# Hybrid decoder layer on one core: residual additions queued behind the local softmax's maxima, local scores in another order, other places for the attention steps

## The chip, the core and the metric

The kernel runs on one core of a Trainium2 chip. The core has five engines that work side by side, each with its own queue of instructions: TensorE (PE, matrix products; its weight loads are shown as PEld), VectorE (DVE), ScalarE (ACT), GpSimd (POOL), and SyncE (SP), which here only issues transfers. [...] Semaphores order the engines among each other. The metric is the device time of one execution in microseconds (us), as the median of several runs.

## The reference

One layer of a hybrid decoder on 4096 new prompt tokens (width 1024) and 8 x 8 sample tokens with caches. Cut to what matters here:

```
h = rmsnorm(x, g_pre);  z = h @ w_in          # 2816 columns: conv, q, k, v, gates
out_a = silu(cg) * cb * conv3(cc * ch)        # 256 columns
# window attention: 8 query heads, 2 key heads, blocks of 128 queries,
# keys of this and of the previous block, a sink logit per head
s = q k^T / 8, masked to the last 128 keys;  m = max(max(s), sink)
p = exp(s - m) / (sum(exp(s - m)) + exp(sink - m));  out_b = silu(ag) * (p v)
# cross attention: 4 heads, 256 memory tokens
out_c = silu(mg) * (softmax(mq mk^T / 8) mv)
y = concat(out_a, out_b, out_c) @ w_out       # 1024 x 1024
x + rmsnorm(y, g_post)
```

Everything is in float32. The kernel keeps this exactness by splitting factors into a high and a low part of the fast float32 format and adding three products (two where it suffices).

## The kernel before

The work has two stages. The first, some 938 us long, is the input projection in three phases over groups of output columns; each phase goes through eight token blocks of 520, each block through seven products of a Strassen scheme (`steps`, line 505). In the third phase the attention of the first chunk (256 tokens) runs between the products, cut in pieces that are taken one per step: `third_jobs` (line 812) gives the step n = 7(b-1)+p its jobs, n = 14 makes the memory's keys (`mem_keys`, whose transposes stand in a PSUM tile until lines 809 and 810 have read it), n = 15 loads chunk 0 (`first_chunk`, line 840), and from n = 16 on one piece of the list `third["chunk"]` is taken per step. The first piece is `chunk.values` (line 849), the transposes of V (line 1117, `vtp`), then come the four head pairs of window and cross attention. When the list is empty, chunk 1 is loaded.

The second stage is the output projection of 33 blocks of 128 tokens (`Block.run`, line 1548): two accumulators `y` of 512 columns, for each of them eight steps of three products (line 1561). Before the products of a step, `starts` may call something (line 1559): here the attention of the later chunks is woven in. A half-block h (128 tokens, chunk h // 2) has two parts. `first_half(h)` (line 1592) takes the window scores (`window_scores`, line 1283: 16 products `ws`, eight over all 128 rows at line 1292, then eight over 64 rows at line 1295), the transposes `xt` of the half-block before (line 1326), then the window softmax of both key heads (`window_probabilities`, line 1299), and it issues loads: for an even h the keys, queries and V of the chunk after (`chunk_load`: ten transfers on GpSimd's queue, one on SP's), for an odd one the gates of the next chunk (`load_mix`, SP). `second_half(h)` (line 1607) takes the memory scores `xs`, the value products `wo` of the half-block before, for an even h V's transposes, then the transposes `wt` of the window probabilities (line 1338), which ScalarE copies (line 1270) and GpSimd masks (lines 1275 and 1278).

The window softmax of a key head is, on VectorE if nothing else is said: copy of the scores (ScalarE, line 1305), masking with the scores of the block before (1306), maximum (1247), its negative with the sink (1249) and the sink's share (1251), exponentials with sums (ScalarE, 1255), sum (1257), reciprocal (1259), multiplication (1260). Both heads go through it one after the other.

Where the parts stand is written in `EARLY` (line 1630) as steps counted from the first block, 16 per block: first and second half of half-block 2 at 4 and 12, of 3 at 14 and 20, of 4 at 22 and 28, of 5 at 30 and 36, and the first half of 6 at 38. From then on every block has a second half at its step 12, and from block 3 on a first half at step 4.

At the end of a block its norm is made: squares (ScalarE, 1569), the sum on VectorE (1574), a power on GpSimd (1575), and the residual on VectorE (1579), which scales `yn`, adds the block's input `xr` in place, and is followed by the store (1580). `yn` has one buffer, `xr` two: the load of a block's rows waits for the store of the block two before.

In this stage TensorE's order is the program's order. The other engines' order is made by a planner, which goes through the work with its own estimate of times and takes, among what it thinks ready, what stands first in the program. `keep_in_program_order(x)` pins x behind the instruction that was written just before it for the same engine.

Of the kernel before, what the change touches and what calls it, by code (L numbers as in the profile page):

```python
# [15 lines left out]
P = 128  # L16
# [36 lines left out]
def hybrid_layer(ctx: ExitStack, tc: tile.TileContext, a: dict):  # L53
# [786 lines left out]
    def first_chunk():  # L840

        mem_stack.close()
        third["work"] = mem_stack.enter_context(tc.tile_pool(name="work", bufs=5, side="right"))
        chunk_load(0)
        chunk = chunks[0]
        chunk.load_mix()
        third["chunk"] = pieces = [lambda: chunk.values(None)]
        for left, right_, both in chunk.pairs():
            pieces += [lambda u=u, n=n: [next(u, None) for _ in range(n)] for n in (2, 1) for u in (left, right_)] + [both]
# [208 lines left out]

    class Chunk:
# [185 lines left out]
        def window_softmax(self, b, kvh, sm):  # L1245
            mx = tiny.tile([P, 4], F32, tag="mx", name=f"wmx{b}_{kvh}")
# [7 lines left out]
            for hh in range(4):  # L1254
                S.activation(sm[:, hh, :], sm[:, hh, :], AF.Exp, bias=nm[:, hh : hh + 1], scale=SCALE,  # L1255
                             accum_out=den[:, hh : hh + 1])
            V.tensor_tensor(den, den, es, op=ALU.add)
# [25 lines left out]
        def window_scores(self, i):  # L1283
            b = 2 * self.c + i
            w = [two_banks("w", f"ws{b}_{kvh}") for kvh in range(2)]
            tasks = [(kvh, j % 2, j // 2) for kvh in range(2) for j in range(4)]
            out = lambda kvh, col, bank: w[kvh][:, bank, 256 * col : 256 * col + 256]
            q = lambda kvh, col, bank: self.q[:, 4 + 2 * (2 * bank + col) + kvh, i * P : i * P + P]
            k = lambda kvh, part: self.kst[:, 2 * kvh + part, i * P : i * P + 2 * P]
            for kvh, col, bank in sorted(tasks):  # L1290

                TE.matmul(out(kvh, col, bank), q(kvh, col, bank), k(kvh, 0), start=col == 0, stop=True, skip_group_check=col > 0)
            for kvh, col, bank in sorted(tasks):
                r = slice(64 * bank, 64 * bank + 64)
                TE.matmul(out(kvh, col, bank), q(kvh, col, bank)[r], k(kvh, 1)[r], start=False, stop=True,
                          skip_group_check=True, tile_position=(64 * bank, 0))
            self.ws = w

        def window_probabilities(self, i):
            b, w = 2 * self.c + i, self.ws  # L1300
            self.sms = []
            for kvh in range(2):
                sm = work([P, 4, P], "sm", f"sm{b}_{kvh}")
# [3 lines left out]
                self.window_softmax(b, kvh, sm)  # L1307
                self.sms.append(sm)
# [212 lines left out]
    class Block:  # L1521
# [26 lines left out]
        def run(self, last, starts):  # L1548
# [6 lines left out]
            for p, (c0, c1) in enumerate(parts):  # L1555
                acc = psum("z", f"y{b}_{p}")[:, : c1 - c0]
                j, passes = 0, 3 if m == P else 2
                for k in range(KT):
                    starts.get((p, k), lambda: None)()
                    for l, r in ((0, 0), (1, 0), (0, 1)) if m == P else ((0, 0), (0, 1)):  # L1560
# [14 lines left out]
            G.tensor_tensor(st[:m, 3:4], st[:m, 3:4], mhalf[:m, 0:1], op=ALU.pow)  # L1575
            if last:
                V.tensor_tensor(yn[:m, 768:D], acc[:m], gpost[:m, 768:D], op=ALU.mult)
            for cs in (slice(0, 512), slice(512, D)) if last else (slice(0, D),):
                V.scalar_tensor_tensor(self.xr[:m, cs], yn[:m, cs], st[:m, 3:4], self.xr[:m, cs], op0=ALU.mult, op1=ALU.add)  # L1579
# [27 lines left out]
    def second_half(h):  # L1607
# [17 lines left out]
        if new_v:  # L1625
            for n in range(2):
# [3 lines left out]
    EARLY = {4: (first_half, 2), 12: (second_half, 2), 14: (first_half, 3), 20: (second_half, 3), 22: (first_half, 4),  # L1630
             28: (second_half, 4), 30: (first_half, 5), 36: (second_half, 5), 38: (first_half, 6)}
# [7 lines left out]
    def run(i, starts):  # L1639
# [12 lines left out]
        blocks[i].run(i == len(blocks) - 1, starts)  # L1652
# [28 lines left out]
    run(32, {})  # L1681
    att.close()
# [105 lines left out]
```

## Time and profile before

| | us |
|---|---|
| runs, median of 3 | 1552.72 (1552.12 to 1554.6) |
| profiled execution | 1562.16 |
| its span, first to last instruction | 1560.3 |
| TensorE busy | 1525.2 (98%) |
| VectorE busy | 1145.7 (73%) |
| ScalarE busy | 792.5 (51%) |
| GpSimd busy | 394.6 (25%) |
| mean granted TensorE clock | 0.994 |

A row of a timeline has start, duration, engine, line, operation, output and inputs by name with their shapes, how many were merged, and in brackets how long the engine stood idle before and what ended that. A row of waits reads: engine, what waited, what it waited for: us in total, how often, the longest. A row of windows has the stretch, its length, the busy time of PE, PEld, DVE, ACT and POOL with their instructions, then the granted TensorE clock (1.00 is full), the busy share of the transfer engines and GB/s. Matrix products overlap each other, so their durations are longer than their spacing.

### The profile page before, as it was taken

To read this page: it belongs to the slowest core of one execution; us is meant where nothing else is said; L and a number is where in the kernel's file an instruction comes from. 1 tells how busy PE (TensorE), PEld (TensorE's weight loads), DVE (VectorE), ACT (ScalarE), POOL (GpSimd) and SP (SyncE) were. 2 spreads that over 40 slices of the span, in tenths; PEclk is the share of its full clock that TensorE was granted. 3 is DMA by queue.
4 is the path that set the end of the run, shared out by engine and by line. 5 is a ranking of instruction groups with operands and counts; after the bars stand their busy time and mean duration, and the time that the engine had idled before them with its cause. 6 is when DMAs were issued, how large, how long until landed. Compare 5 with 4: busy or idle time off the path is not lost. (4 is left out here: it accounts for less than half of the span.)

```text
span 1560.3 us, 30035 instructions
## 1 busy us (share of the span) xinstructions
PE 1525.2 (98%) x11341; PEld 1391.5 (89%) x11341; DVE 1145.7 (73%) x1965; ACT 792.5 (51%) x1949; POOL 394.6 (25%) x635
## 2 busy tenths in 40 slices
PE   9999999999999999999999999999999999999998
PEld 9999999999999999999999997788777777777766
DVE  5779887899888777986677687766666666666643
ACT  6776666475222222454354355755555555555532
POOL 0222322221300000000101105544444444444410
PEclk9999999999999999999999999999999999999999
DMA  9989999878755333788867869976777777776322
GB/s 260 169 233 223 284 281 260 278 246 274 190 178 178 124 124 124 252 267 268 229 233 211 265 244 302 184 146 146 147 156 156 150 154 150 158 152 146 119 96 95
DMA packets 178453, 306.28 MB, mean 196 GB/s; under 512 B 34437, under 2 KB 108165, under 8 KB 178277
## 3 DMA queue, kind: packets, MB, share of 16 engines
q1 hardware_dynamic: 130901, 227.38, 47.8%
q0 software_dynamic: 46688, 75.93, 24.4%
q8 instruction: 90, 1.47, 0.4%
q10 hardware_dynamic: 720, 1.05, 0.2%
q14 instruction: 54, 0.44, 0.1%
HBM read 197.23 MB, written 108.05 MB: 196 GB/s over the span
## 5 line engine op out<-in xcount | busy, mean ns | idle before, releaser
L1561 PE MATMUL y<-wo,mh 128*128 128x512 f32 (+1 forms) x1040 | 338.9, 396 | 0.0
L375 DVE TENSOR_TENSOR z<-c,z 128x520 f32<-128x520 f32 (+1 forms) x308 | 194.4, 644 | 88.3 <-PE c L368 84.1
L1561 PEld LDWEIGHTS y<-wo,mh 128*128 128x128 f32 x1040 | 195.6, 189 | 40.8 <-issue 2.0
L1561 PE MATMUL y<-wo,ml 128*128 128x512 f32 (+1 forms) x520 | 202.0, 388 | 0.0
L1161 POOL TENSOR_SCALAR xp<-xp,xrd 128x256 f32<-128x256 f32 x128 | 60.2, 480 | 251.9 <-DVE xrd L1153 250.1
L1561 PEld LDWEIGHTS y<-wo,ml 128*128 128x128 f32 x520 | 98.7, 190 | 17.9
L1255 ACT ACTIVATE sm<-sm,wnm 128x128 f32<-128x128 f32 x256 | 99.2, 389 | 25.9 <-DVE wnm L1249 25.8
L1152 ACT ACTIVATE xp<-xs,xnm 128x256 f32<-128x256 f32 x128 | 59.5, 470 | 88.0 <-DVE xnm L1150 85.4
L1092 POOL DMA_DIRECT2D q<-qd x96 | 60.3, 637 | 108.3 <-DVE wo L186 60.4
L1579 DVE SCALAR_TENSOR_TENSOR xr<-yn,yst,xr 128x1024 f32<-128x1024 f32 (+2 forms) x34 | 42.5, 1253 | 50.3 <-POOL yst L1575 50.3
L1330 ACT COPY xpt<-xt 128x512 f32<-128x512 f32 x30 | 17.6, 587 | 109.1 <-DVE xpt L1330 109.1
L737 POOL CAST wmask<-negs 128x256 uint8<-128x256 f32 x1 | 1.2, 1227 | 265.3 <-DMA negs<-in_wmask 265.3
L1278 POOL TENSOR_SCALAR_AFFINE_SELECT wpt<-wpt 128x512 f32<-128x512 f32 x64 | 56.5, 893 | 42.7 <-ACT wpt L1270 42.4
L1568 DVE TENSOR_TENSOR yn<-y,gpost 128x512 f32<-128x512 f32 (+1 forms) x66 | 44.7, 677 | 21.4 <-PE y L1561 21.1
L276 ACT ACTIVATE nat<-nat 104x1024 f32<-104x1024 f32 x40 | 42.3, 1058 | 27.7 <-DMA nat<-in_x_p 27.5
L1275 POOL TENSOR_SCALAR_AFFINE_SELECT wpv<-wpt 128x512 f32<-128x512 f32 x62 | 51.0, 837 | 6.3 <-ACT wpt L1270 6.3
L1153 DVE RECIPROCAL xrd<-xden 128x2 f32<-128x2 f32 x64 | 10.6, 166 | 56.6 <-ACT xp L1152 56.6
L377 ACT COPY z<-c 128x520 f32<-128x520 f32 (+1 forms) x44 | 24.3, 553 | 51.6 <-PE c L368 48.5
L1338 PE MATMUL wt<-ident,sm 128*128 128x128 f32 x240 | 36.6, 281 | 14.2 <-DVE sm L1260 11.7
L407 ACT CAST zh<-z 128x520 fp32r<-128x520 f32 x56 | 33.4, 625 | 33.2 <-DVE z L375 29.5
L1569 ACT ACTIVATE y<-y 128x512 f32<-128x512 f32 (+1 forms) x66 | 38.9, 589 | 19.5 <-DVE yn L1568 19.5
L1338 PEld LDWEIGHTS wt<-ident,sm 128*128 128x128 f32 x240 | 26.2, 142 | 24.9 <-ACT y L1569 14.6
(978 smaller groups left out, 5191.8 us busy)
## 6 DMA issues: line engine op xcount, KB each, us to landing
q<-qd POOLq DMA_DIRECT2D x96, 256.0 KB, 6.6
xr<-in_x_p SPq DMA_DIRECT2D x32, 512.0 KB
nat<-in_x_p SPq DMA_DIRECT2D x39, 416.0 KB
o_yp<-xr SPq DMA_DIRECT2D x31, 512.0 KB
md<-th POOLq DMA_DIRECT2D x48, 260.0 KB, 6.6
qd<-zh SPq DMA_DIRECT2D x48, 260.0 KB
qd<-z SPq DMA_DIRECT2D x48, 260.0 KB
kst<-qd POOLq DMA_DIRECT2D x60, 192.0 KB, 4.7
```

The lines of the kernel that those rows point to most:

```text
L276: S.activation(t[:RG], t[:RG], AF.Square, accum_out=r[:RG, i : i + 1])
L375: add = lambda dst, other: V.tensor_tensor(dst, c, other, op=ALU.add)
L1092: G.dma_start(self.q[64 * half : 64 * half + 64, i : i + 4, :].rearrange("p (j v) n -> p j v n", v=2), heads(part, j, self.ts))
L1152: S.activation(p[:, i, :], s[:, i, :], AF.Exp, bias=nm[:, i : i + 1], scale=SCALE, accum_out=den[:, i : i + 1])
L1161: G.tensor_scalar(p[:, i, :], p[:, i, :], self.rds[h][:, i : i + 1], 0.5, op0=ALU.mult, op1=ALU.mult)
L1255: S.activation(sm[:, hh, :], sm[:, hh, :], AF.Exp, bias=nm[:, hh : hh + 1], scale=SCALE, accum_out=den[:, hh : hh + 1])
L1275: G.affine_select(pv.rearrange("p (h q) -> p h q", h=4), p3, pattern=[[0, 4], [-1, P]], compare_op=ALU.is_gt, fill=0.0, base=0, channel_mu ...
L1278: G.affine_select(p3, p3, pattern=[[0, 4], [1, P]], compare_op=ALU.is_ge, fill=0.0, base=0, channel_multiplier=-1)
L1338: TE.transpose(tw[:, kvh, hh * P : (hh + 1) * P], self.sms[kvh][:, hh, :], ident)
L1561: TE.matmul(acc, self.hl[l][:, k], wo[k][c0 // 512][:, r, c0 % 512 : c0 % 512 + c1 - c0], start=j == 0, stop=j == passes * KT - 1)
L1568: V.tensor_tensor(yn[:m, c0:c1], acc[:m], gpost[:m, c0:c1], op=ALU.mult)
L1579: V.scalar_tensor_tensor(self.xr[:m, cs], yn[:m, cs], st[:m, 3:4], self.xr[:m, cs], op0=ALU.mult, op1=ALU.add)
```

## The change

Four things are changed.

1. `Block.run` no longer ends with the residual. It returns it as a function, `finish`, kept in `left[0]`; `finish_block` carries it out once. In `window_probabilities` the softmax is cut in two: `window_exps` (maxima to exponentials) for both heads, then `finish_block(True)`, then `window_shares` (sum, reciprocal, multiplication) for both. There the residual is pinned behind the last VectorE instruction before it, which is the second head's line 1251. Where no such first half has come by step 5 of the next block, the residual is taken there unpinned, and after the last block at the end.
2. `window_scores` issues the 16 products by key head: four full and four 64-row products of the first head, then four 64-row and four full ones of the second.
3. `EARLY` has other steps: 4 and 15 for half-block 2, 17 and 22 for 3, 24 and 28 for 4, 31 and 37 for 5, 40 for the first half of 6.
4. An empty piece is put ahead of `chunk.values`, so chunk 0's pieces all come one step of the third phase later.

```diff
-        third["chunk"] = pieces = [lambda: chunk.values(None)]
+        third["chunk"] = pieces = [lambda: None, lambda: chunk.values(None)]
...
+    left = [lambda queued: None]
+
+    def finish_block(queued=False):
+
+        fn, left[0] = left[0], lambda queued: None
+        fn(queued)
...
         def window_softmax(self, b, kvh, sm):
+            self.window_shares(b, kvh, sm, *self.window_exps(b, kvh, sm))
+
+        def window_exps(self, b, kvh, sm):
             mx = tiny.tile([P, 4], F32, tag="mx", name=f"wmx{b}_{kvh}")
...
+            return den, es
+
+        def window_shares(self, b, kvh, sm, den, es):
             V.tensor_tensor(den, den, es, op=ALU.add)
...
-            for kvh, col, bank in sorted(tasks):
-
-                TE.matmul(out(kvh, col, bank), q(kvh, col, bank), k(kvh, 0), start=col == 0, stop=True, skip_group_check=col > 0)
-            for kvh, col, bank in sorted(tasks):
-                r = slice(64 * bank, 64 * bank + 64)
-                TE.matmul(out(kvh, col, bank), q(kvh, col, bank)[r], k(kvh, 1)[r], start=False, stop=True,
-                          skip_group_check=True, tile_position=(64 * bank, 0))
+            for kvh, part in ((0, 0), (0, 1), (1, 1), (1, 0)):
+                for _, col, bank in sorted(t for t in tasks if t[0] == kvh):
+                    r = slice(64 * bank, 64 * bank + 64) if part else slice(0, P)
+                    place = {"tile_position": (64 * bank, 0)} if part else {}
+
+                    first = part == kvh and col == 0
+                    TE.matmul(out(kvh, col, bank), q(kvh, col, bank)[r], k(kvh, part)[r], start=first, stop=True,
+                              skip_group_check=not first, **place)
...
-            self.sms = []
-            for kvh in range(2):
-                sm = work([P, 4, P], "sm", f"sm{b}_{kvh}")
+            self.sms = [work([P, 4, P], "sm", f"sm{b}_{kvh}") for kvh in range(2)]
+            for kvh, sm in enumerate(self.sms):
...
-                self.window_softmax(b, kvh, sm)
-                self.sms.append(sm)
+            dens = [self.window_exps(b, kvh, sm) for kvh, sm in enumerate(self.sms)]
+            finish_block(True)
+            for kvh, sm in enumerate(self.sms):
+                self.window_shares(b, kvh, sm, *dens[kvh])
...
+                    if (p, k) == (0, 5):
+                        finish_block()
...
+            return lambda queued: self.finish(last, yn, st, acc, dst, queued)
+
+        def finish(self, last, yn, st, acc, dst, queued):
+            m = self.m
...
-                V.scalar_tensor_tensor(self.xr[:m, cs], yn[:m, cs], st[:m, 3:4], self.xr[:m, cs], op0=ALU.mult, op1=ALU.add)
+                x = V.scalar_tensor_tensor(self.xr[:m, cs], yn[:m, cs], st[:m, 3:4], self.xr[:m, cs], op0=ALU.mult, op1=ALU.add)
+                if queued:
+                    tc.keep_in_program_order(x)
...
-    EARLY = {4: (first_half, 2), 12: (second_half, 2), 14: (first_half, 3), 20: (second_half, 3), 22: (first_half, 4),
-             28: (second_half, 4), 30: (first_half, 5), 36: (second_half, 5), 38: (first_half, 6)}
+    EARLY = {4: (first_half, 2), 15: (second_half, 2), 17: (first_half, 3), 22: (second_half, 3), 24: (first_half, 4),
+             28: (second_half, 4), 31: (first_half, 5), 37: (second_half, 5), 40: (first_half, 6)}
...
-        blocks[i].run(i == len(blocks) - 1, starts)
+        left[0] = blocks[i].run(i == len(blocks) - 1, starts)
...
     run(32, {})
+    finish_block()
```

## The prediction

> **What bounds the kernel now.** I read the page's busy shares first, then the waits of TensorE, then those waits by stage, then the windows, and last the instructions of one steady block in order of time. The first row is the page's, the second stands in the waits of the whole run, the next five in the waits of 937 to 1010 us (first blocks of the output projection), one in those of 1095 to 1445, the last two in those of 1445 to the end. Between 1010 and 1095 the view has no row.
>
> ```profile
> PE 1525.2 (98%) x11341; PEld 1391.5 (89%) x11341; DVE 1145.7 (73%) x1965; ACT 792.5 (51%) x1949; POOL 394.6 (25%) x635
> ...
> PE vtp L1117 <- DVE mk L810: 2.6, 1, 2.6
> ...
> PE wt L1338 <- ACT sm L1255: 1.7, 1, 1.7
> PE ws L1292 <- ACT wpt L1270: 1.1, 1, 1.1
> PE xt L1326 <- ACT xp L1152: 1.1, 1, 1.1
> PE wt L1338 <- DVE sm L1260: 1.0, 2, 0.6
> PE ws L1292 <- DVE mix L1354: 0.5, 1, 0.5
> ...
> PE wt L1338 <- DVE sm L1260: 10.7, 19, 0.8
> ...
> PE xt L1326 <- DVE mix_s L1434: 2.0, 1, 2.0
> PE wt L1338 <- ACT sq L1411: 0.8, 1, 0.8
> ```
>
> TensorE is the bound: 98% busy, and the change neither adds nor removes a matrix product. So the time can move only by TensorE's waits and by its clock. The reader is to see three places: one wait in the third phase (2.6), five kinds in the first blocks (5.4), and 19 waits of one kind in the steady blocks (10.7), all for the window softmax (`sm`).
>
> The windows show what the clock adds (the column after POOL's is the granted clock):
>
> ```profile
> 784.00:788.00 4.00, 4.00 (x24) 4.00 (x25) 2.06 (x3) 1.51 (x3) 0.00 (x0) 0.63 0.81 322
> 788.00:792.00 4.00, 4.00 (x34) 4.00 (x34) 1.98 (x3) 1.61 (x3) 0.00 (x0) 0.95 0.49 143
> ...
> 952.00:954.00 2.00, 1.76 (x7) 1.60 (x8) 1.28 (x4) 1.36 (x6) 0.93 (x2) 0.56 1.15 380
> 954.00:956.00 2.00, 2.00 (x8) 1.61 (x7) 0.17 (x1) 1.35 (x5) 1.99 (x4) 0.58 1.78 260
> ```
>
> Right behind the 2.6 us wait the clock loses (1-0.63)x4 + (1-0.95)x4 = 1.7 us, and right behind the waits of 1.7 and 0.6 us at 949 to 952 it loses (0.44+0.42)x2 = 1.7 us again. [...]
>
> One steady block in order of time (start us, us, engine):
>
> ```profile
> 1201.45 1.11 PE L1292 MATMUL ws<-kst,q 128*128 128x256 f32 x8
> 1202.49 0.74 PE L1295 MATMUL ws<-kst,q 64*128 64x256 f32 x8
> 1203.04 1.07 ACT L1305 COPY sm<-ws 128x512 f32<-128x512 f32 x2 [0.29 <-PE ws L1295]
> 1203.37 0.20 DVE L1574 TENSOR_SCALAR yst<-yst 128x1 f32<-128x1 f32 x1
> 1202.32 2.21 POOL L1278 TENSOR_SCALAR_AFFINE_SELECT wpt<-wpt 128x512 f32<-128x512 f32 x2
> 1204.51 0.56 POOL L1575 TENSOR_TENSOR yst<-yst,mhalf 128x1 f32<-128x1 f32 x1
> 1205.10 1.28 DVE L1579 SCALAR_TENSOR_TENSOR xr<-yn,yst,xr 128x1024 f32<-128x1024 f32 x1 [1.53 <-POOL yst L1575]
> 1206.31 1.33 DVE L1306 COPY_PREDICATED sm<-wmask,ws 128x512 f32<-128x512 uint8 x2
> 1208.13 1.26 DVE L1247 TENSOR_REDUCE wmx<-sm 128x4 f32<-128x512 f32 x2
> 1209.31 0.28 DVE L1249 SCALAR_TENSOR_TENSOR wnm<-wmx,nsink 128x4 f32<-128x4 f32 x2
> 1209.71 0.68 DVE L1568 TENSOR_TENSOR yn<-y,gpost 128x512 f32<-128x512 f32 x1
> 1211.28 0.16 DVE L1257 TENSOR_TENSOR wden<-wden,wes 128x4 f32<-128x4 f32 x1 [0.88 <-ACT sm L1255]
> 1212.91 0.16 DVE L1257 TENSOR_TENSOR wden<-wden,wes 128x4 f32<-128x4 f32 x1 [0.53 <-ACT sm L1255]
> 1213.32 0.69 DVE L1260 TENSOR_TENSOR sm<-sm,wrd 128x512 f32<-128x512 f32 x1
> 1213.09 0.66 PE L1338 MATMUL wt<-ident,sm 128*128 128x128 f32 x4
> 1214.16 0.63 PE L1338 MATMUL wt<-ident,sm 128*128 128x128 f32 x4 [0.42 <-DVE sm L1260]
> ```
>
> VectorE has the scores' copies from 1203.6 on (half of ScalarE's 1.07), but at the head of its queue stands the residual L1579, which waits for GpSimd's power L1575, which stands behind GpSimd's mask L1278. So the masking L1306 begins at 1206.31, and the softmax's last multiplication ends at 1214.01, 0.3 us after TensorE could have taken it (1213.09+0.66).
>
> **The steady blocks.** What do these waits cost? The window transposes of three blocks give the period:
>
> ```profile
> 1026.99 1.09 PE L1338 MATMUL wt<-ident,sm 128*128 128x128 f32 x8
> 1063.30 1.09 PE L1338 MATMUL wt<-ident,sm 128*128 128x128 f32 x8
> ...
> 1175.32 0.66 PE L1338 MATMUL wt<-ident,sm 128*128 128x128 f32 x4
> ```
>
> Without a wait two blocks take 1063.30-1026.99 = 36.31 us, with waits 1213.09-1175.32 = 37.77: 0.73 per block, a little more than the waits shown (10.7/19 = 0.56), since the stream also fills anew. Eighteen and a half blocks lie between 1095 and 1445: 13.5 us to be had, 10.7 by the rows of waits alone.
>
> The residual moves behind both heads' maxima. Its 1.28 us is moved, not removed. The masking can begin at 1203.6, 2.7 us earlier. Behind the maxima VectorE waits for the exponentials, 0.88+0.53 us in the rows; the residual's 1.28 and the L1568 that is there already may push the second multiplication by 0.5 at most. So `sm` ends at 1214.01-2.7+0.5 = 1211.8, 1.9 us before TensorE wants it. The loop softmax, cross softmax, masks on GpSimd, power, residual, masking runs beside TensorE at 37.77/2 = 18.9 us per block; it falls to about 16.7, under TensorE's 18.16. Late next is TensorE itself. I take the whole 13.5. Queued behind the residual are now only sums, reciprocals and multiplications of the softmax, and its input L1575 ends at 1205.07, two us before the maxima will. On SP the store of the result and, behind it, the load of the next residual's rows go 2 us later; they are wanted two blocks on, so I cost them at nothing. L1568 needs the buffer that the residual reads, at 1209.71, after the residual's new end at about 1208.4: nothing, while that cover holds; without it L1568 and a block's accumulator wait.
>
> **The scores group by group.** The same 16 products in another order. Full and 64-row forms change twice per step before (eight, eight, then the full transposes) and twice after (four, eight, four): nothing on TensorE, bounds 0 and plus or minus 0.1 per block, 3 us over 30, since the rows show no gap between L1292 and L1295. It lets ScalarE copy the first head some 0.9 us earlier (half of 1203.23-1201.45); this is room, not a term.
>
> **The places.** A step of three output products:
>
> ```profile
> 1204.01 0.48 PE L1561 MATMUL y<-wo,mh 128*128 128x512 f32 x1
> 1209.58 0.63 PE L1317 MATMUL xs<-mk,q 128*128 128x256 f32 x4
> ...
> 970.20 0.74 PE L1295 MATMUL ws<-kst,q 64*128 64x256 f32 x8
> 978.47 0.69 DVE L1260 TENSOR_TENSOR sm<-sm,wrd 128x512 f32<-128x512 f32 x1
> ```
>
> Eight steps lie between the first two rows, so one is 0.7 us. The second half of half-block 2 goes from step 12 to 15: 2.1 us of products against waits of 1.7+0.6; 0.4 stays. The first halves at 14, 22, 30, 38 go to 17, 24, 31, 40, the second ones at 20, 28, 36 to 22, 28, 37. From first to second half there are now 11, 5, 4, 6, 4 steps instead of 8, 6, 6, 6, 6. Eight steps leave 1213.75-1203.23 = 10.5 us from the scores' end to the second head's transposes, so four leave 7.7. In the first blocks the softmax takes 979.16-970.94 = 8.2, less some of the 0.9 above: 0.3 for each of the two four-step places. The waits of 1.1 for `wpt` and 1.1 for `xp` get a step more and keep 0.4 each; the one of 0.5 keeps 0.2. The first transposes of `xp` lose the half clock that hid their factors: I charge one wait like the row, 1.0. Sum 0.4+0.6+0.8+0.2+1.0 = 3.0 of 5.4, so 2.4 less, and 1.7 of clock: 4.1. Bounds: all of 5.4+1.7 = 7.1 gained; or 4.7 lost (below). Each moved first half takes along its loads, ten on GpSimd's queue and V's on SP, or the mix's on SP; from load to use chunk 3 keeps 16 steps (24 to 40, 22 to 38 before), so they cost nothing; if they came late, TensorE would wait at the scores.
>
> **V's first transposes** go one step of the third phase later, 36 products, over 4 us: more than the wait of 2.6, so I take it away with its 1.7 of clock: 4.3. All 21 later pieces of chunk 0 and the load of chunk 1 go with it, some 40 us before chunk 1 is read. No row shows another wait among them; bounds 4.3 gained and 4.3 lost, if one piece falls onto the same kind of stall.
>
> **The last blocks** (2.8 us of waits) I leave as they are: between 3.7 gained, should the residual fall behind what L1434 needs, and 1.3 lost, one residual.
>
> Sum: 13.5 + 4.1 + 4.3 = 21.9 us. The profiled execution took 1562.16 us, 9.4 over the median of the runs; it would take 1540.3. On the median of 1552.72 it is 1530.8, say 1531.
>
> **The rivals.** (A) *The short places stall.* If the softmax takes as long there as in the steady block, 1214.01-1203.23 = 10.8, four steps leave 3.1 us of wait twice, each followed by 1.7 of clock: 9.6 instead of 0.6, so 12.9 gained, 1540. For it: VectorE is 78% busy (56.9 of 73 us) there; against it: the 8.2 row.
>
> ```profile
> 937.00:1010.00 73.00, 67.43 (x437) 52.80 (x436) 56.94 (x135) 45.78 (x168) 38.68 (x66) 0.98 1.15 256
> ```
>
> (B) *V's wait only moves*: 4.3 less, 1535. (C) *The clock's windows stay*, for another cause than the waits: 3.4 less, 1534. [...] (D) *The change doesn't do what it says*: another link, the split or the masks on GpSimd, still holds the loop at 18.9; only 8.4 is gained, 1544. Against it: 2.7 us of the loop are idle or residual. (E) *Slower: the residual blocks VectorE.* If GpSimd's power came late, the residual would stand at the head of VectorE's queue with the softmax's sums behind it. From the power's end to `sm` are then 1.28 + 2.2 (two times sum, reciprocal, multiplication), so up to a power that ends at 1210.2 nothing is lost, 5.1 us later than the row; each us beyond costs 25 us over the 25 blocks that queue it. It decides from 1211.0 on; at 1211.7 the kernel takes 1531+38 = 1569. [...] Against it: GpSimd has only the mask ahead of the power.
>
> **How the numbers follow.** Forecast 0.50, A 0.15, B 0.10, C 0.05, D 0.07, no change 0.04, E 0.09. What a measurement can tell is about 0.2%, 3.1 us: faster 0.87, same 0.04, slower 0.09. The range starts at 1531 less 3.7 (last blocks) and 3.0 (no wait left in the first), 1524, and reaches D's 1544 and the 1.3 of the last blocks, 1546.
>
> **What would show it.** After: no `wt` wait for L1260 from 1090 on and periods of 36.3 us per two blocks; the residual behind the maxima, not waiting for L1575; no `vtp` wait and no clock under 1 near 785 and 953; small waits near 955 to 1010. Wrong would make it: waits of 2 to 3 us before `wt` in blocks 1 and 2, new waits for accumulators in the third phase, or idle VectorE before L1579's successor.

## The result, and the profile after

| | before | after |
|---|---|---|
| runs, median of 6 each, side by side | 1553.04 us (1551.9 to 1555.49) | 1533.84 us (1532.58 to 1539.86) |
| profiled execution | 1562.16 us | 1536.39 us |
| mean granted TensorE clock in it | 0.994 | 0.999 |

The ratio is 0.9881, with a 95% interval of 0.9863 to 0.9899: 19.2 us faster (1553.04 - 1533.84). 1531 was forecast. The two profiled executions differ by 25.8, more than the runs do, because the one of before lay 9.4 over its median and the one of after 2.5; so what is read from the two traces alone is too large by some 6.6 us.

The busy shares on the page of the changed kernel (its span is 1534.7 us):

```profile
PE 1516.2 (99%) x11341; PEld 1387.8 (90%) x11341; DVE 1151.6 (75%) x1965; ACT 797.7 (52%) x1949; POOL 393.1 (26%) x635
```

The waits of TensorE, in the first blocks (three rows, 925 to 1010 us) and at the end (one row, 1425 to 1545). Between 700 and 925 and between 1010 and 1425 the view has no row at all; 1095 to 1425 held 9.9 us in 18 waits before.

```profile
PE wt L1353 <- DVE sm L1273: 2.2, 2, 1.3
PE wt L1353 <- DVE xrd L1160: 0.6, 2, 0.4
PE ws L1309 <- PE y L1578: 0.5, 1, 0.5
...
PE xt L1341 <- DVE mix_s L1449: 0.6, 1, 0.6
```

The windows at the two places where the clock had been low before (the granted clock stands behind POOL's column):

```profile
784.00:788.00 4.00, 4.00 (x35) 4.00 (x35) 2.34 (x5) 1.51 (x3) 0.00 (x0) 1.00 0.56 179
...
952.00:954.00 2.00, 1.88 (x13) 1.38 (x12) 1.79 (x3) 0.68 (x2) 2.00 (x5) 1.00 1.10 322
```

To see where the time went, the second stage is cut at rows of TensorE: its first output product, and the window transposes `wt` of half-blocks 6, 11, 28 and 29, and its last product. Before:

```profile
937.93 0.39 PE L1561 MATMUL y<-wo,mh 128*128 128x512 f32 x1
1009.01 1.04 PE L1338 MATMUL wt<-ident,sm 128*128 128x128 f32 x8
1099.73 0.66 PE L1338 MATMUL wt<-ident,sm 128*128 128x128 f32 x4
1420.94 0.60 PE L1338 MATMUL wt<-ident,sm 128*128 128x128 f32 x4
1440.21 0.66 PE L1338 MATMUL wt<-ident,sm 128*128 128x128 f32 x4
1552.83 0.28 PE L1561 MATMUL y<-wo,mh 128*128 128x256 f32 x1
```

and after:

```profile
933.21 0.39 PE L1578 MATMUL y<-wo,mh 128*128 128x512 f32 x1
1000.90 0.60 PE L1353 MATMUL wt<-ident,sm 128*128 128x128 f32 x4
1092.15 1.09 PE L1353 MATMUL wt<-ident,sm 128*128 128x128 f32 x8
1401.16 1.04 PE L1353 MATMUL wt<-ident,sm 128*128 128x128 f32 x8
1419.17 1.09 PE L1353 MATMUL wt<-ident,sm 128*128 128x128 f32 x8
1527.10 0.28 PE L1578 MATMUL y<-wo,mh 128*128 128x256 f32 x1
```

| stretch, between these rows | before | after | gain |
|---|---|---|---|
| up to the first output product | 937.93 | 933.21 | 4.7 |
| first blocks, to `wt` of half-block 6 | 71.08 | 67.69 | 3.4 |
| half-blocks 6 to 11 | 90.72 | 91.25 | -0.5 |
| 17 steady half-blocks, 11 to 28 | 321.21 | 309.01 | 12.2 |
| half-block 28 to 29 | 19.27 | 18.01 | 1.3 |
| from there to the end of the last product | 112.90 | 108.21 | 4.7 |

The sum is 25.7. A steady half-block takes 309.01/17 = 18.18 us, TensorE's own 18.16 within what a row can tell. In order of time it now looks like this:

```profile
1189.85 0.56 POOL L1592 TENSOR_TENSOR yst<-yst,mhalf 128x1 f32<-128x1 f32 x1
1191.24 0.74 DVE L1319 COPY_PREDICATED sm<-wmask,ws 128x512 f32<-128x512 uint8 x1 [1.72 <-ACT sm L1318]
1193.21 0.73 DVE L1319 COPY_PREDICATED sm<-wmask,ws 128x512 f32<-128x512 uint8 x1
1193.83 0.15 DVE L1259 SCALAR_TENSOR_TENSOR wnm<-wmx,nsink 128x4 f32<-128x4 f32 x1
1195.01 1.28 DVE L1600 SCALAR_TENSOR_TENSOR xr<-yn,yst,xr 128x1024 f32<-128x1024 f32 x1
1198.22 0.69 DVE L1273 TENSOR_TENSOR sm<-sm,wrd 128x512 f32<-128x512 f32 x1
1201.15 1.09 PE L1353 MATMUL wt<-ident,sm 128*128 128x128 f32 x8
```

The masking starts with the first head's copy, the residual (L1600) stands behind both maxima and waits for nothing, the power (L1592) having ended 4.6 us before it. The last multiplication ends at 1198.91; TensorE takes the second head's transposes after four of the eight, at about 1201.8, so 2.9 us of room stand where 0.3 us were missing.

### The profile page after: what moved, and what is told of

Same layout as the page of the kernel before. It is cut to its first block, busy times and chain, and to the rows that moved or that the text cites. A ratio compares the mean times of both kernels' runs of the same rounds, so it can differ in the third digit from the quotient of the medians.

```text
span 1534.7 us, 30061 instructions
## 1 busy us (share of the span) xinstructions
PE 1516.2 (99%) x11341; PEld 1387.8 (90%) x11341; DVE 1151.6 (75%) x1965; ACT 797.7 (52%) x1949; POOL 393.1 (26%) x635
## 4 chain that ended last, share of the span: by engine, by line
PE 68%; DMA 13%; DVE 9%; issue 5%; ACT 2%; POOL 1%; SPq 1%; ACTq 0%; DVEq 0%; POOLq 0%
PE c L368 33%; PE y L1578 21%; PE ws L1309 3%; PE wo L1057 2%; DMA place<-in_xt 2%; PE wt L1353 2%; PE xs L1332 2%; PE xt L1341 1%; PE wo L1218 1%; DMA nat<-in_x_p 1%; DVE z L375 1%; PE wo L1224 1%; DMA wr_3A<-in_w_in 1%; DMA zs<-qd 1%; DMA md<-th 1%
## 5 line engine op out<-in xcount | busy, mean ns | idle before, releaser
L1319 DVE COPY_PREDICATED sm<-wmask,ws 128x512 f32<-128x512 uint8 x60 | 43.9, 735 | 49.3 <-ACT sm L1318 49.2
L1291 POOL TENSOR_SCALAR_AFFINE_SELECT wpt<-wpt 128x512 f32<-128x512 f32 x64 | 64.9, 1033 | 43.4 <-ACT wpt L1283 43.1
L1318 ACT COPY sm<-ws 128x512 f32<-128x512 f32 x60 | 35.1, 586 | 65.0 <-PE ws L1309 65.0
L1309 PEld LDWEIGHTS ws<-kst,q 128*128 128x128 f32 (+1 forms) x480 | 50.3, 187 | 12.0 <-PE y L1578 0.9
L1309 PE MATMUL ws<-kst,q 128*128 128x256 f32 (+1 forms) x480 | 59.5, 299 | 0.8 <-PE y L1578 0.5
L407 ACT CAST zh<-z 128x520 fp32r<-128x520 f32 x56 | 33.3, 624 | 35.0 <-DVE z L375 31.9
L1086 POOL DMA_DIRECT2D kst<-qd x64 | 38.7, 617 | 42.9 <-issue 24.5
L1265 ACT ACTIVATION_READ_ACCUMULATOR sm<-sm,wnm 128x1 f32 x256 | 47.8, 187 | 0.0
```

What stands on the lines that cost most here:

```text
L1291: G.affine_select(p3, p3, pattern=[[0, 4], [1, P]], compare_op=ALU.is_ge, fill=0.0, base=0, channel_multiplier=-1)
L1319: V.copy_predicated(sm4, third["wmask"].unsqueeze(1).to_broadcast([P, 2, 2, P]), s4[:, :, :, 0:P])
```

## The experiments

Each kernel is timed against runs of the kernel before on the same chip, whose medians were 1553.01 to 1554.36 us; so times from different chips compare to about 1.4 us, and the ratios are the safer figures. The stretches are from one profiled execution each. The columns of the table: the 17 steady half-blocks and the first blocks, cut at the same rows as above, and the stretch from half-block 29 to the end.

| kernel | median, us | ratio to before, 95% | 17 steady | first blocks | end |
|---|---|---|---|---|---|
| after | 1533.84 | 0.9863 to 0.9899 | 309.0 | 67.7 | 108.2 |
| *one part undone* | | | | | |
| score order old | 1535.89 | 0.9847 to 0.9896 | 308.7 | 67.7 | 107.8 |
| places old | 1533.15 | 0.9836 to 0.9884 | 309.0 | 68.8 | 107.9 |
| V's transposes old | 1534.61 | 0.9842 to 0.9892 | 309.0 | 67.7 | 107.9 |
| residual at once | 1544.36 | 0.9908 to 0.9952 | 310.3 | 75.3 | 111.8 |
| residual at once but in block 0 | 1541.60 | 0.9905 to 0.9939 | 310.9 | 69.2 | 111.4 |
| residual queued, not pinned | 1543.01 | 0.9917 to 0.9951 | 310.3 | 72.1 | 111.8 |
| residual and softmax old | 1540.36 | 0.9899 to 0.9926 | 309.0 | 73.8 | 109.5 |
| *one part alone* | | | | | |
| residual queue alone | 1532.94 | 0.9850 to 0.9884 | 308.7 | 69.5 | 107.8 |
| score order alone | 1538.34 | 0.9890 to 0.9928 | 309.0 | 71.8 | 109.1 |
| places and V alone | 1556.56 | 1.0002 to 1.0021 | 321.2 | 72.9 | 113.2 |
| *after, with more on VectorE* | | | | | |
| one more ahead of each residual | 1531.48 | 0.9840 to 0.9867 | 309.0 | 67.7 | 107.9 |
| three more | 1556.61 | 1.0006 to 1.0030 | 323.5 | 69.7 | 109.7 |

The theory at the start was the prediction's: the steady blocks run at the length of a loop over VectorE, ScalarE and GpSimd, and the residual ahead of the masking is what makes it longer than TensorE's 18.16 us. The rival: another part of the change holds the gain, or the parts stand in for one another.

### One part undone at a time

The residual at once: the changed kernel with the residual carried out right behind each block's norm, as before.

```diff
         left[0] = blocks[i].run(i == len(blocks) - 1, starts)
+        finish_block()
```

> The changed kernel with the residual carried out at the end of its own block again; scores group by group, new places and V's shift stay. If the queued residual brings the steady gain: the window transposes wait for the softmax again, 0.4 to 0.7 us per block from about 1090 us on, periods of 37.7 us per two blocks instead of 36.3, 12 to 14 us slower than the changed kernel (about 1547 us). If it was the earlier scores of the first head that brought it: no such waits, about 1534 us.

The other three undo the order of the scores (the loop over `sorted(tasks)` is back), the steps of `EARLY`, and the empty piece ahead of V's first transposes.

```diff
-            for kvh, part in ((0, 0), (0, 1), (1, 1), (1, 0)):
...
+            for kvh, col, bank in sorted(tasks):
...
-    EARLY = {4: (first_half, 2), 15: (second_half, 2), 17: (first_half, 3), 22: (second_half, 3), 24: (first_half, 4),
...
+    EARLY = {4: (first_half, 2), 12: (second_half, 2), 14: (first_half, 3), 20: (second_half, 3), 22: (first_half, 4),
...
-        third["chunk"] = pieces = [lambda: None, lambda: chunk.values(None)]
+        third["chunk"] = pieces = [lambda: chunk.values(None)]
```

> The changed kernel with the sixteen score products in the old order (eight full, eight 64-row). If the order is only room: within 1.5 us of the changed kernel (1534 us), no new waits in the steady blocks, since the softmax there ends 2.9 us before TensorE wants it. If the order carries a part of the gain: waits in the first blocks grow and the time is 3 us or more above 1534. If the extra change of form costs TensorE 0.1 us per block: 3 us faster.

> The changed kernel with the old places of the halves (4, 12, 14, 20, 22, 28, 30, 36, 38). If the places are worth what the prediction says: 3 to 4 us slower than the changed kernel (about 1537.5 us), a wait of 1.5 us or more near 949 us and a half clock window behind it. If the queued residual alone had cured the first blocks too: within 1 us of 1534 us and no such wait.

> The changed kernel with V's first transposes one step earlier again. If the wait costs its length and a half clock window: 4.3 us slower than the changed kernel (about 1538 us), a wait of 2.6 us near 783 us and a clock of 0.63 in the 4 us behind it. If the wait costs its length alone: 2.6 us slower, clock 1.0. If the wait was an accident of the one profiled execution: no difference.

Undoing the scores' order, the places or V's place changes the time by nothing that can be told (1535.89, 1533.15, 1534.61). Only with the residual at once does the time change, and then 10 us of the gain are lost, not 20: most of the steady loss did not return (310.3 us for 17 half-blocks, not 321). This contradicted the loop as the prediction had it, for here the residual is ahead of the masking again and waits for the power:

```profile
1194.74 0.67 DVE L1585 TENSOR_TENSOR yn<-y,gpost 128x512 f32<-128x512 f32 x1
1199.84 1.28 DVE L1600 SCALAR_TENSOR_TENSOR xr<-yn,yst,xr 128x1024 f32<-128x1024 f32 x1 [1.52 <-POOL yst L1592]
1201.04 0.73 DVE L1319 COPY_PREDICATED sm<-wmask,ws 128x512 f32<-128x512 uint8 x1
1203.01 0.73 DVE L1319 COPY_PREDICATED sm<-wmask,ws 128x512 f32<-128x512 uint8 x1
1203.63 0.15 DVE L1259 SCALAR_TENSOR_TENSOR wnm<-wmx,nsink 128x4 f32<-128x4 f32 x1
1207.64 0.69 DVE L1273 TENSOR_TENSOR sm<-sm,wrd 128x512 f32<-128x512 f32 x1
```

What differs from before is VectorE's order behind the residual. Before, the planner put both maskings ahead of both maxima; the first exponentials' bias (L1249) came 4.2 us after the residual's start (1209.31 - 1205.10) and the last multiplication ended 8.9 us after it (1214.01 - 1205.10). Here the first head goes through masking and maximum before the second head's masking; the bias comes at 3.8 and the end at 8.5 (1208.33 - 1199.84). These 0.4 us are the larger part of what the loop lost (18.9 to 18.25 us per half-block); where the rest went was not followed.

### The residual queue alone, and the score order alone

So two parts may each do the same. The first kernel is the changed one with the other three parts undone (the split of the softmax belongs to the queue and stays); the second is the kernel before with the new order of the products. Of each edit the first lines are shown.

```diff
-            for kvh, part in ((0, 0), (0, 1), (1, 1), (1, 0)):
...
+            for kvh, col, bank in sorted(tasks):
...
-    EARLY = {4: (first_half, 2), 15: (second_half, 2), 17: (first_half, 3), 22: (second_half, 3), 24: (first_half, 4),
...
+    EARLY = {4: (first_half, 2), 12: (second_half, 2), 14: (first_half, 3), 20: (second_half, 3), 22: (first_half, 4),
...
-        third["chunk"] = pieces = [lambda: None, lambda: chunk.values(None)]
+        third["chunk"] = pieces = [lambda: chunk.values(None)]
```

```diff
-            for kvh, col, bank in sorted(tasks):
...
+            for kvh, part in ((0, 0), (0, 1), (1, 1), (1, 0)):
...
```

> The changed kernel with the old order of the scores, the old places and V's first transposes where they were: only the residual is queued behind the maxima (and the local softmax is split for it). If that one part carries the gain, as the three runs with one part undone suggest, the time is 1533 to 1537 us and 17 steady blocks take 308.5 to 309.5 us. If the other three parts stand in for one another, so that undoing one alone showed nothing, it is 1540 to 1547 us.

> The kernel before with the new order of the local scores alone; the residual stays at once. If finishing the first head's scores early lets VectorE take its maximum ahead of the second masking, and so shortens the loop from the residual to the second head's weights, 17 steady blocks take 310 to 315 us instead of 321 and the time is 1543 to 1548 us. If the order of the scores does nothing by itself, the time is 1552 to 1556 us and the 17 blocks take 320 to 322 us.

The queue alone takes 1532.94 us: the whole gain, as its first theory had it. The score order alone takes 1538.34, better than its expectation (1543 to 1548): 15 of the 20 us, with the steady blocks at 309.0. The parts overlap, and their gains must not be added.

How can two orders that keep the residual ahead of the masking differ, 309.0 here and 310.3 above? The groups of VectorE in the steady stretch show it (1095 to 1425; busy time, mean ns of one, idle time ahead of it and what ended that). Before, and after:

```profile
L1568 DVE TENSOR_TENSOR yn<-y,gpost 128x512 f32<-128x512 f32 x35 | 23.7, 677 | 0.0
L1579 DVE SCALAR_TENSOR_TENSOR xr<-yn,yst,xr 128x1024 f32<-128x1024 f32 x17 | 21.8, 1285 | 31.9 <-POOL yst L1575 31.9
```

```profile
L1319 DVE COPY_PREDICATED sm<-wmask,ws 128x512 f32<-128x512 uint8 x36 | 26.5, 736 | 34.0 <-ACT sm L1318 34.0
L1585 DVE TENSOR_TENSOR yn<-y,gpost 128x512 f32<-128x512 f32 x37 | 25.6, 691 | 31.9 <-PE y L1578 31.3
...
L1600 DVE SCALAR_TENSOR_TENSOR xr<-yn,yst,xr 128x1024 f32<-128x1024 f32 x18 | 23.1, 1284 | 0.3 <-issue 0.3
```

the residual at once, and the score order alone:

```profile
L1585 DVE TENSOR_TENSOR yn<-y,gpost 128x512 f32<-128x512 f32 x36 | 24.5, 679 | 0.4 <-PE y L1578 0.4
...
L1600 DVE SCALAR_TENSOR_TENSOR xr<-yn,yst,xr 128x1024 f32<-128x1024 f32 x18 | 23.1, 1284 | 33.6 <-POOL yst L1592 33.6
```

```profile
L1569 DVE TENSOR_TENSOR yn<-y,gpost 128x512 f32<-128x512 f32 x37 | 25.4, 687 | 24.7 <-PE y L1562 24.7
L1580 DVE SCALAR_TENSOR_TENSOR xr<-yn,yst,xr 128x1024 f32<-128x1024 f32 x18 | 23.1, 1284 | 27.6 <-POOL yst L1576 27.6
```

The scaling `yn` needs TensorE's finished accumulator. Where VectorE waits there (24.7, 31.3), TensorE sets the pace. Where it hardly ever waits (0.0, 0.4), TensorE's accumulator is always there already, and the other engines' loop sets the pace. All fourteen traces divide this way: 11 us of waiting or more where the 17 half-blocks take 308.7 or 309.0, at most 1.3 where they take longer. The idle time ahead of the residual says nothing of this: it is about 30 us in three of the four. With the residual at once the loop is just too long, 310.3/17 = 18.25 us against 18.18. With the score order alone it is just short enough, and the row that differs is the first bias, which comes 3.2 us after the residual's start, ahead of the second masking:

```profile
1189.45 1.28 DVE L1580 SCALAR_TENSOR_TENSOR xr<-yn,yst,xr 128x1024 f32<-128x1024 f32 x1 [1.53 <-POOL yst L1576]
1190.65 0.72 DVE L1307 COPY_PREDICATED sm<-wmask,ws 128x512 f32<-128x512 uint8 x1
1192.62 0.15 DVE L1249 SCALAR_TENSOR_TENSOR wnm<-wmx,nsink 128x4 f32<-128x4 f32 x1
1192.68 0.73 DVE L1307 COPY_PREDICATED sm<-wmask,ws 128x512 f32<-128x512 uint8 x1
1197.04 0.69 DVE L1260 TENSOR_TENSOR sm<-sm,wrd 128x512 f32<-128x512 f32 x1
```

The end is at 8.3 (1197.73 - 1189.45), 0.2 less than with the residual at once.

### Is it the split softmax?

By that reading the residual at once loses its steady time because the split softmax, a part that goes with the queue, puts the first bias behind the second masking. A kernel with both the residual and the softmax of before, and all else of the change:

```diff
-            dens = [self.window_exps(b, kvh, sm) for kvh, sm in enumerate(self.sms)]
-            finish_block(True)
-            for kvh, sm in enumerate(self.sms):
-                self.window_shares(b, kvh, sm, *dens[kvh])
+                self.window_softmax(b, kvh, sm)
...
-        left[0] = blocks[i].run(i == len(blocks) - 1, starts)
+        blocks[i].run(i == len(blocks) - 1, starts)
```

> The changed kernel with both the residual and the local softmax as before; the new order of the scores, the places and V's transposes stay. If the run with the residual at once alone lost steady time because the split softmax put the first head's bias (the smaller of the sink and the maximum) behind the second head's masking, the loop is 17.8 us here, under TensorE's 18.16: 17 blocks take 309 us, the stretch after them 108 to 109 us, and the time is 1536 to 1540 us. If the residual at once loses it in any case, 17 blocks take 310.3 us or more and the time is 1542 to 1546 us.

It takes 1540.36 us, with 309.0 in the steady blocks and VectorE waiting again 23.5 us for TensorE's accumulators. So this is shown: the split softmax costs the 1.3 us there when the residual stands ahead. That it does so by the place of the first bias is read from rows: here the bias comes 3.2 us after the residual's start again (1196.44 - 1193.27), ahead of the second masking (1196.51). What is left against the changed kernel, 6.5 us, lies by the profiles almost all in the first blocks (73.8 against 67.7).

### The first blocks: rows that come late

With the residual at once, the first block's residual stood at the head of VectorE's queue until its input rows were there. The load, the residual, and the wait of TensorE that follows:

```profile
951.52 0.88 SPq L1545 DMA_DIRECT2D xr<-in_x_p  x2
957.62 1.28 DVE L1600 SCALAR_TENSOR_TENSOR xr<-yn,yst,xr 128x1024 f32<-128x1024 f32 x1 [5.38 <-DMA xr<-in_x_p]
...
960.78 1.44 PE L1332 MATMUL xs<-mk,q 128*128 128x256 f32 x5 [3.38 <-ACT xpt L1345]
```

Test: the residual at once in every block but the first.

```diff
         left[0] = blocks[i].run(i == len(blocks) - 1, starts)
+        if i > 0:
+            finish_block()
```

> The changed kernel with the residual at once in every block but the first, which keeps it behind the maxima. If the residual at once lost its 10 us because the first block's residual stood 5.4 us for its input rows at the head of VectorE's queue, the first blocks take about 68 us again and the time is 1536 to 1539 us. If the loss is spread over all blocks or comes from the clock, it stays at 1542 to 1546 us.

In the profile the first blocks are back at 69.2 us (from 75.3): the wait of 3.38 us is gone, and so are 5.1 us lost to the half clock (0.50 granted), 3.4 from 959.4 to 966.2, which began during that wait, and 1.7 behind another wait, which both traces have (1.68 us, at 998.8 and at 994.0); other waits are 1.4 us longer. In the runs the two kernels can't be told apart (0.9905 to 0.9939 against 0.9908 to 0.9952), so how much the late rows cost in the median is not shown. The time is 1541.6, above the range: of the 7.8 us over the changed kernel, the traces show 1.5 in the first blocks, 1.9 in the 17 steady ones, and 3.2 at the end. The expectation had put too much of the loss on one block.

And the queued residual without its pin:

```diff
-                if queued:
-                    tc.keep_in_program_order(x)
```

> The changed kernel without the lines that keep the queued residual behind the maxima in program order: the scheduler then puts it ahead of the maskings again in some of the first blocks and nowhere else. If the first blocks are where the order matters, they lose as with the residual at once, 3 to 10 us: 1537 to 1544 us. If it is the steady blocks alone that the order serves, the time is 1533 to 1536 us.

1543.01 us. The expectation rested on a wrong premise: the trace shows the residual ahead of the maskings in nearly every block, its 18 in the steady stretch standing 33.5 us for the power; in the first blocks TensorE stands 3.56 us ahead of the memory scores `xs` at 957.48, the wait that was 3.38 us with the residual at once. Without the pin the planner undoes the queue; the pin carries it.

The places, which bring this stall about, were then run without the queue, V's transposes with them:

```diff
-    EARLY = {4: (first_half, 2), 12: (second_half, 2), 14: (first_half, 3), 20: (second_half, 3), 22: (first_half, 4),
...
+    EARLY = {4: (first_half, 2), 15: (second_half, 2), 17: (first_half, 3), 22: (second_half, 3), 24: (first_half, 4),
...
-        third["chunk"] = pieces = [lambda: chunk.values(None)]
+        third["chunk"] = pieces = [lambda: None, lambda: chunk.values(None)]
```

> The kernel before with the other places of the first and second halves and V's first transposes one step later, and nothing else. By the prediction's two terms (4.1 and 4.3) it would take 1544 to 1546 us. If their waits were the accident of one execution, as the changed kernel with the one or the other undone suggests, it is 1551 to 1555 us; the 17 steady blocks take 320 to 322 us either way.

1556.56 us, 0.02% to 0.21% slower than before. Half-block 3's first half, three steps later, lets block 0's residual go ahead of its masking, and there it stands:

```profile
955.27 1.28 DVE L1579 SCALAR_TENSOR_TENSOR xr<-yn,yst,xr 128x1024 f32<-128x1024 f32 x1 [4.91 <-DMA xr<-in_x_p]
...
958.44 1.21 PE L1317 MATMUL xs<-mk,q 128*128 128x256 f32 x8 [2.89 <-ACT xpt L1330]
```

### How much room is behind the maxima

One and three more VectorE instructions, which change no value, ahead of each queued residual (the edit with three):

```diff
             for cs in (slice(0, 512), slice(512, D)) if last else (slice(0, D),):
+            for _ in range(3 if queued else 0):
+                tc.keep_in_program_order(V.scalar_tensor_tensor(yn[:m], yn[:m], 1.0, yn[:m], op0=ALU.mult, op1=ALU.max))
```

> The changed kernel with one more VectorE instruction of 1.28 us, which changes no value, ahead of each queued residual. By the loop worked out from the trace (15.8 us per block against TensorE's 18.16) there is room for it: 1533 to 1537 us. If each us behind the maxima costs TensorE a us, it is 1.28 x 25 = 32 us more, 1566.

> The same with three such instructions, 3.84 us: the loop becomes 15.8 + 3.84 = 19.6 us, 1.5 over TensorE's 18.16, so some 25 blocks lose 30 to 40 us and the waits for the second head's multiplication are back: 1564 to 1576 us. If work behind the maxima is hidden whatever its length, it stays below 1540 us.

One costs nothing: 1531.48 us, 309.0 in the steady blocks, with VectorE's waits for TensorE's accumulators down from 31.3 to 11.3. Three cost 22.8 us (1556.61 - 1533.84), less than the expectation, whose 15.8 us for the loop of the changed kernel were too long: measured are 323.5/17 = 19.03 us with the three, so 15.4 without them. The 2.9 us of room read above give it better: 3 x 1.22 = 3.66, so 0.8 us per half-block is missing; measured are (323.5 - 309.0)/17 = 0.85. VectorE never waits for an accumulator again, and the multiplication is late as before the change:

```profile
1201.27 1.22 DVE L1598 SCALAR_TENSOR_TENSOR yn<-yn 128x1024 f32<-128x1024 f32 x1
...
1208.06 0.68 DVE L1273 TENSOR_TENSOR sm<-sm,wrd 128x512 f32<-128x512 f32 x1
...
1208.88 0.63 PE L1353 MATMUL wt<-ident,sm 128*128 128x128 f32 x4 [0.79 <-ACT y L1586]
```

(The wait is put down to ScalarE's `y`, but the transposes read `sm`, whose multiplication ends 0.1 us before them.)

No kernel is clearly faster than the changed one: the queue alone, the changed kernel with the old places, and the one with one more instruction overlap it in their intervals.

## Why the prediction came out right, point by point

The time, 1533.84, lies 3 us from the forecast of 1531 and inside the range; the gain in the runs is 19.2 us against 21.9. But the sum is nearer than its terms: two of them, 8.4 us together, gave nothing that the runs show, and gains that had been put at nothing made up for them. That part is luck.

**Steady blocks, 13.5.** Right in size and place: 12.2 + 1.3 = 13.5 us in the two stretches from half-block 11 to 29. "No `wt` wait from 1090 on" holds. The part of the loss that the waits did not show (0.73 against 0.56 us per block) stands in TensorE's busy time before: the same 231 products take 36.31 us of it in the two blocks without a wait and 36.70 in the two with, at full clock in both. In place of 1.9 us of room there are 2.9: relative to the first score product, the last multiplication ends at 9.4 (1198.91 - 1189.51) instead of 12.6 (1214.01 - 1201.45), 3.2 earlier where 2.2 was expected. The loop was the right mechanism, and its price behind the break-even, "25 us per us", stood the test: 0.76 us too much would be 19, measured were 22.8.

**The scores group by group, 0.** The number holds once the residual is queued (undone: 1535.89, not distinguishable). The step "this is room, not a term" fails for the part by itself: alone it gave 15 us. By the rows it does not act through the 0.9 us of an earlier copy (ahead of its maskings, which read the copies, VectorE has no idle time in the steady stretch); it turns VectorE's order round, first head's maximum before the second head's masking, and that takes enough out of the same loop. A loop that is 0.7 us over its bound is cured by either of two cuts, and the second is worth nothing.

**The places, 4.1.** Failed. With the old places back, the time does not change (1533.15), though the row that the term was built on does come back: the wait of 1.73 us, at 945.4, and a half clock from 946.4 to 949.8. The first blocks of that profile are only 1.1 us longer (68.8 against 67.7) and the half-blocks 6 to 11 behind them 0.6 us shorter. The step that failed is the comparison with the waits of the kernel before. The new places leave 2.2 + 0.6 + 0.5 = 3.3 us of waits, much as predicted (3.0), though at other instructions (1.3 us at half-block 2, where 0.4 was charged, and 0.9 at half-block 3, where nothing was), and no half clock. But beside the queue the old places leave only 2.9 us and 1.7 of half clock, not 5.4 and 1.7. So 1.3 us were to be had, not 4.1, and in the runs not even these show. Without the queue the places even do harm: put into the kernel before together with V's place, they make it 2.5 us slower, since they move the first block's residual ahead of a masking, onto rows that arrive late. "They cost nothing" was said of the loads that move along; the residual's own rows were not looked at. The queue hides this stall.

**V's first transposes, 4.3.** Failed as a term: the wait of 2.6 us belonged to one execution. With V's transposes in their old place the profiles show this wait at 0.3 us (V's transposes old), at 1.0 us (queue alone) and not at all (score order alone), none of them with a half clock there, and the first output product comes at 928.98 us with the queue alone, earlier than the 933.21 of the changed kernel. What made it so long in that one execution is not settled.

**The last blocks, 0.** Mis-sized, and outside its bound of 3.7: 4.7 us by the profiles, of which some 3 are waits (2.0 + 0.8 + 0.8 + 0.2 before, 0.6 after) and 1.7 the half clock behind the wait of 2.0, (0.26 + 0.50 + 0.10) x 2 by the granted clocks of 0.74, 0.50 and 0.90 in the windows from 1494 to 1500. The queue alone has it too (107.8), so it takes no more than the residual. Without the half clock it would be 3.0 and inside the bound. Together with the steady blocks this term makes 18.2 us by the profiles, and the first blocks add 3.4; with the -0.5 of half-blocks 6 to 11 that is 21.1, more than the 19.2 of the runs, so a part of it belongs to the one execution that was profiled.

**The rivals.** A: the two places of four steps (half-blocks 4 and 6) kept waits of 0.2 and 0.4 us, near the 0.3 that was charged for each, in place of 3.1 (the view puts them down to `xrd`, but the transposes read `sm`, whose multiplication ends 0.15 us before them); the 1.3 and 0.9 us left stand at half-blocks 2 and 3. B and C: no new wait and no half clock in the third phase, but what they argued about was one execution. D: did not happen; yet with the residual at once the split softmax does hold the loop at 18.25, so "another link" was not far. E: the power ended 4.6 us before the residual wanted it. Its price is confirmed by the three extra instructions, and its form (a residual at the head of the queue, with ready work behind it) is what the residual at once shows in block 0, for late rows in place of a late power. There the first head's scores lay ready while VectorE stood 5.38 us.

## What to carry to other kernels

Look for the instruction that waits at the head of its engine's queue with ready work behind it, and move it behind work that can't start sooner anyway; look at all its inputs, since in the first block the residual's late rows (5.38 us with the residual at once), not the power (31.9/17 = 1.9 us per steady half-block before), were the larger stall. Whether a loop over other engines or the bounding engine set the pace could be read here from the idle time ahead of the instruction that takes the bounding engine's result: at most 1.3 us over the 17 half-blocks where it was the loop, 11 or more where it was TensorE. Gains of parts that shorten the same loop are not added, and a wait seen in one execution is no term of a sum.

## What was not expected of the hardware

TensorE's half clock did not follow the length of a wait. The same wait in the same place, 1.73 us, was followed by it in one kernel (the queue alone, where it ended at 942.1) and not in another (the score order alone, where it ended at 941.4).

The records of the granted clock show where it begins. In every one of these traces that has more than one stretch at half clock they begin on a grid of 3.413 us, and ahead of the last product they last one step of it, or two. In the kernel before they begin at 88.69, 785.01, 952.26 and 1494.98 us, which lie 204, 49 and 159 times 3.4133 us apart. Where the grid lies differs between the profiled executions (half clocks begin at 944.21 with the queue alone and at 946.4 with the old places). In these traces the half clock goes with how long TensorE stood idle within one step. The two kernels, cut at the grid (in the second its place is taken from the half clock that begins at 988.77), the queue alone first:

```profile
940.79:944.21 3.42, 1.55 (x10) 1.30 (x11) 2.72 (x10) 3.23 (x15) 0.39 (x1) 1.00 1.20 376
944.21:947.62 3.41, 3.41 (x13) 2.92 (x11) 0.70 (x3) 1.74 (x6) 3.41 (x8) 0.50 1.36 303
```

```profile
937.57:940.98 3.41, 2.12 (x15) 1.72 (x13) 2.63 (x11) 3.09 (x17) 0.01 (x1) 1.00 1.25 370
940.98:944.39 3.42, 2.40 (x14) 2.02 (x15) 2.46 (x7) 3.23 (x13) 1.25 (x3) 1.00 1.18 378
```

With the queue alone, 3.42 - 1.55 = 1.87 us of idle time fall into one step (most of this wait and the next one, of 0.59 us), and the next step runs at half clock, a loss of 3.41 x 0.50 = 1.7 us. With the score order alone the grid cuts the wait in two: 1.29 and 1.02 us fall into two steps, and neither slows the step behind it (1.00 in the second row, and in the step after it).

From 780 us to the last product, over all fourteen traces, each cut at its own grid, and by the rows of TensorE, a half clock followed all eight full-clock steps with 1.96 us or more of idle time, four of the seven with 1.63 to 1.92, and none of those with 1.56 or less. In the kernel before this idle time was 2.30, 2.33 and 1.96 us of the 3.41 in the steps ahead of 785.01, 952.26 and 1494.98. What decides between 1.63 and 1.92 stays open: the wait of 1.80 us near 1450 lies within one step both with the residual at once, where the half clock follows (0.73 and 0.50 in the next two windows of 2 us), and with the residual at once but in block 0, where it doesn't (1.00 throughout). A wait of 2.89 us (places and V alone), which the grid cuts into 1.77 and 1.12, had none behind it.

So in these traces a wait of about 2 us cost its own length, and 1.7 us more (3.41 x 0.50) for the step at half clock that followed twelve of the fifteen steps with 1.63 us or more of idle time. The profiled execution of the kernel before has four half-clock steps ahead of its last product (6.8 us), that of the changed kernel none. In the runs the difference is smaller: the mean granted clock was 0.997 over the 43 timed runs of the kernel before beside the experiments and 0.999 in each of the six of the changed kernel, some 3 us (0.002 x 1553 = 3.1). With the 2.6 us wait of V's transposes, 6.8 - 3.1 + 2.6 = 6.3 us, this is an estimate of most of the 6.6 us by which the profiles differ more than the runs.
